# Ten products over a blank tile, in place of twenty, ahead of the first dense product of a two-layer encoder kernel

## The chip, the core and the metric

One core of one Trainium2 chip runs the whole program. The metric is the device time of one execution, in microseconds (us), as the median of several runs.

## The reference, cut to what matters

One sequence of 512 tokens of width 1024 goes through two layers. The first is a Mamba-2 mixer (a state-space scan in chunks), the second a differential attention. The change lies ahead of the first layer's first projection. What is computed there and right behind it is this:

```python
h = rms_norm(x, norm_g)
zxbcdt = h @ w_in                       # z, then x/B/C, then dt
z, xbc, dt_raw = ...
xbc = jax.nn.silu(causal_depthwise_conv(xbc, conv_w, conv_b))
dt = jax.nn.softplus(dt_raw + dt_bias)
y = ssd_chunked_scan(xs * dt[..., None], -jnp.exp(a_log) * dt, bm, cm)   # cumsum of a*dt, exp of its differences
y = gated_group_rms_norm(y + d_skip * xs, z, gate_norm_g)
x = x + y @ w_out
```

Everything is float32. The second layer (a shared K/V projection, eight heads of attention with two softmax maps each, an output projection, a last norm) isn't touched.

## The kernel before, in words

**Products in three parts.** Each dense product is made of three in a faster format: both operands are split into a high part and the rest, and TensorE (PE) computes high by high, high by rest and rest by high (`mm3`). ScalarE (ACT) writes the high part of the weights (`whi`) and VectorE (DVE) the rest (`wlo`), in four pieces of 128x512 for each load of weights (`raw`, 1 MB, sent from SyncE's queue). `raw` has two buffers, `whi` and `wlo` three, so the pieces of the sixth load (called raw5 below) can only be written once PE has finished with those of the third. For the input, `a_hi` and `a_lo` are the same two parts of x transposed (`xt`).

**The head of the program.** `blank` is a 128x128 tile of zeros. A loop multiplies it with itself into a PSUM bank that nobody reads (`warm`), while the first weights and inputs are still in transfer; each such product shows as two rows in the trace. Then come the products of `pz0`: four tiles of 128 tokens by 8 slices of the width by 3, 96 in all.

```python
    V.memset(blank, 0.0)
    ...
    warm = ss_bank("warm")
    for i in range(20):
        T.matmul(warm[:, 0:P], lhsT=blank, rhs=blank, start=True, stop=True)
```

**Behind it.** The squares of x give the norm's factors (`scales`, with `ar_col` by token and `ar_row` along a row). `z_out` takes each `pz` bank to SBUF through SiLU (`zs`). A small product, `ps_dt`, gives dt's raw values; then DVE and ACT compute softplus by a series: `pre` (scaled, biased), `e` (its exponential on ACT), `q` and a chain of eight steps on `pl`, then `pre` again, `q` (a times dt) and the cumulative sum along the chunk, a scan into `e`, which the code calls `acs`. From it ACT makes one more exponential (`toe`, in the tile `q`), and SyncE sends it to DRAM and back, spread over all partitions (`acs_d`, then `dec`). GpSimd (POOL) and ACT make the decays of it.

**The first group.** PE goes on with the projection of group 0 (`pg`: four tiles by 8 slices by 3, 96 products, 48 with one load of weights and 48 with the next). Inside it stand three transposes, `ps_tt`, whose operands are `pre`, `acs` and `toe`. Their place in PE's queue is fixed: after 22 steps, 66 products, of group 0.

```python
    def turned():
        yield "tt"
        ps_tt = ss_bank("ps_tt")
        for i, src in enumerate((dtp, acs, toe)):
            T.transpose(ps_tt[:, i * P:(i + 1) * P], src, ident)
    ...
    T.on = True
    resume(0, 0, turned(), {"tt": 22})
    first_layer()
```

A finished `pg` tile goes through `conv`: DVE multiplies by `ar_row`, ACT starts `xc`, DVE adds three shifted products, ACT takes SiLU. `pxt` are transposes of two such results, further back in PE's queue.

**What sets the order.** Each engine works through its own list in order. Where `T.on` (or `V.on`, `A.on`) is set, the list keeps the order of the code. Elsewhere a scheduler chooses the order when the program is built, after times of its own. In the head and in the first layer PE keeps the code's order from `ps_dt` on, while ACT, DVE, SyncE and the first 96 products of PE are the scheduler's to order. So a change of a loop's count can move instructions far from it.

Nearly all lines go through a helper that records each operation, so they stand under L70, and tiles tell them apart.

Of the kernel before, what the change touches and what calls it, by code (L numbers as in the profile page):

```python
# [78 lines left out]
def trunk(ctx, tc, x, x_t, par, w_dt, w_in, w_out, w_kvqg, w_bo, d_skip, lam_qk, fin_g, out):  # L79
# [16 lines left out]
    def ss_bank(name):  # L96
        turns[0] += 1
        tag = "mm" if turns[0] % turns[1] >= 3 else "ss"
        return psum.tile([P, 512], F32, tag=tag, name=name, bufs=3 if tag == "ss" else 4)
# [290 lines left out]


    warm = ss_bank("warm")
    for i in range(20):
        T.matmul(warm[:, 0:P], lhsT=blank, rhs=blank, start=True, stop=True)
    xt = [bp2.tile([P, 2, S], F32, tag="yl", name=f"xt{i}", bufs=4) for i in range(4)]

# [829 lines left out]
```

## Time and profile before

| | us |
|---|---|
| median of 3 runs (707.1 to 707.22) | 707.15 |
| the profiled execution | 707.6 |
| its span, first to last instruction | 705.8 |
| PE busy (share of the span) | 698.2 (99%) |
| DVE busy | 524.3 (74%) |
| ACT busy | 426.8 (60%) |
| POOL busy | 114.9 (16%) |

The span leaves out 1.8 us of the profiled execution that lie around it. A busy share says for which part of the span an engine had an instruction running. PE's rows overlap their neighbours, since a product is still draining when the next begins; so the distance from start to start tells what one costs, and the busy share tells only that PE stood still nowhere for long.

### The profile page before, as it was taken

How to read it: one execution, taken by the hardware profiler on the slowest of the kernel's cores; microseconds unless marked ns; L12 is line 12 of the kernel's file. 1: busy time of each engine (PE TensorE's matmuls, PEld its weight loads, DVE VectorE, ACT ScalarE, POOL GpSimd, SP SyncE). 2: the span in 40 equal slices, each digit the busy share in tenths (PEclk: the TensorE clock that was granted, in tenths of full speed). 3: DMA queues.
4: the chain of work that ended last, by engine and by line, in shares of the span. 5: the costliest groups of instructions: out<-in, count | busy, mean ns of one | idle time of the engine just before them, and what ended most of it. 6: DMA issues, size and time to landing. Idle time of an engine off the chain costs nothing.

```text
span 705.8 us, 10517 instructions
## 1 busy us (share of the span) xinstructions
PE 698.2 (99%) x3861; PEld 584.5 (83%) x3861; DVE 524.3 (74%) x1184; ACT 426.8 (60%) x930; POOL 114.9 (16%) x154
## 2 busy tenths in 40 slices
PE   9999999999999999999999999999999999999996
PEld 8888888888888888888888888888888888888884
DVE  5599957789489679569996757557778757787776
ACT  6859564484653737536635158567777667665546
POOL 0008241602405025042110101000000000000002
PEclk9999999999999999999999999999999999999999
DMA  8653313314024223313123111513112221130003
GB/s 297 254 208 153 123 57 120 119 61 179 23 97 181 72 107 120 110 71 119 60 67 114 60 59 51 197 60 114 66 60 75 79 87 60 60 107 14 30 1 119
DMA packets 13491, 70.85 MB, mean 100 GB/s; under 512 B 1792, under 2 KB 3328, under 8 KB 6016
## 3 DMA queue, kind: packets, MB, share of 16 engines
q1 hardware_dynamic: 13008, 69.90, 27.5%
q8 instruction: 30, 0.49, 0.3%
q10 hardware_dynamic: 432, 0.28, 0.1%
q14 instruction: 21, 0.17, 0.1%
HBM read 68.02 MB, written 2.16 MB: 99 GB/s over the span
## 4 chain that ended last, share of the span: by engine, by line
PE 93%; DVE 2%; ACT 1%; issue 1%; DMA 1%; POOL 1%; ACTq 0%; POOLq 0%; SPq 0%
PE pg L70 21%; PE po L70 16%; PE pz L70 12%; PE pt L70 8%; PE pq L70 6%; PE pk L70 6%; PE pv L70 6%; PE pb L70 3%; PE sc L70 3%; PE pyd L70 2%; PE pc L70 2%; PE warm L70 1%; PE pyt L70 1%; PE pxt L70 1%; PE psA L70 1%
## 5 line engine op out<-in xcount | busy, mean ns | idle before, releaser
L70 DVE SCALAR_TENSOR_TENSOR wlo<-raw,prm,whi 128x512 fp32r<-128x512 f32 (+1 forms) x240 | 149.0, 672 | 52.4 <-ACT whi L70 52.1
L70 ACT ACTIVATE whi<-raw,prm 128x512 fp32r<-128x512 f32 (+1 forms) x240 | 133.2, 629 | 44.8 <-PE pg L70 13.7
L70 PE MATMUL pg<-a_hi,whi 128*128 128x512 f32 x256 | 102.6, 401 | 0.0
L70 PE MATMUL pg<-a_hi,wlo 128*128 128x512 f32 x256 | 99.8, 390 | 0.0
L70 PE MATMUL pg<-a_lo,whi 128*128 128x512 f32 x256 | 99.8, 390 | 0.0
L70 DVE SCALAR_TENSOR_TENSOR xc<-pg,prc,xc 128x511 f32<-128x511 f32 (+2 forms) x96 | 71.1, 745 | 13.0 <-ACT xc L70 11.8
L70 PEld LDWEIGHTS pg<-a_hi,wlo 128*128 128x128 f32 x256 | 48.0, 188 | 10.2
L70 PEld LDWEIGHTS pg<-a_hi,whi 128*128 128x128 f32 x256 | 48.1, 188 | 9.7 <-issue 0.2
L70 PEld LDWEIGHTS pg<-a_lo,whi 128*128 128x128 f32 x256 | 48.1, 188 | 9.4
L70 PE MATMUL po<-whi,yh 128*128 128x512 f32 x128 | 51.2, 400 | 0.0
L70 PE MATMUL pz<-whi,a_hi 128*128 128x512 f32 x128 | 50.5, 396 | 0.0
L70 PE MATMUL po<-whi,yl 128*128 128x512 f32 x128 | 49.9, 390 | 0.0
L70 PE MATMUL po<-wlo,yh 128*128 128x512 f32 x128 | 49.9, 389 | 0.0
L70 PE MATMUL pz<-whi,a_lo 128*128 128x512 f32 x128 | 49.9, 389 | 0.0
L70 PE MATMUL pz<-wlo,a_hi 128*128 128x512 f32 x128 | 49.8, 389 | 0.0
L1031 POOL TENSOR_TENSOR ot<-x_tok,fg 128x512 f32<-128x512 f32 x4 | 5.0, 1299 | 246.9 <-DVE x_tok L70 246.9
L70 ACT ACTIVATE xc<-xc 128x512 f32<-128x512 f32 x32 | 20.2, 631 | 38.3 <-DVE xc L70 34.4
L70 DVE CUSTOM_DVE_ANT_0 s<-sc,bias 128x128 f32<-128x128 f32 (+3 forms) x64 | 29.4, 488 | 16.0 <-PE sc L70 15.5
L70 ACT ACTIVATE s<-s,mx 128x128 f32<-128x128 f32 (+3 forms) x64 | 35.6, 557 | 9.1 <-DVE mx L70 8.9
L70 ACT ACTIVATE xc<-pg,prc 128x512 f32<-128x512 f32 x32 | 24.8, 774 | 26.3 <-DVE pg L70 24.5
L656 POOL TENSOR_TENSOR xe<-xdt,tok 128x256 f32<-128x256 f32 x24 | 14.1, 613 | 159.3 <-DVE xdt L70 159.3
L70 ACT ACTIVATE tmp<-dx 128x256 f32<-128x256 f32 x32 | 13.2, 412 | 44.2 <-DVE dx L70 44.2
(239 smaller groups left out, 1657.7 us busy)
## 6 DMA issues: line engine op xcount, KB each, us to landing
raw<-in_w_in SPq DMA_DIRECT2D x22, 1024.0 KB, 4.9
raw<-in_w_kvqg SPq DMA_DIRECT2D x16, 1024.0 KB, 4.8
dec<-acs_d SPq DMA_DIRECT2D x8, 1024.0 KB, 4.8
raw<-in_w_out SPq DMA_DIRECT2D x8, 1024.0 KB, 4.9
raw<-in_w_bo SPq DMA_DIRECT2D x4, 1024.0 KB, 4.8
x_tok<-in_x SPq DMA_DIRECT2D x4, 512.0 KB, 9.1
out<-ot SPq DMA_DIRECT2D x6, 256.0 KB, 2.1
raw<-in_w_in SPq DMA_DIRECT2D x4, 256.0 KB, 4.7
```

What stands on the lines that cost most here:

```text
L70: i = op(*args, **kw)
L656: GP.tensor_tensor(out=xe[:, c], in0=xdt[:, c], in1=toe_tok[:, c, hs].unsqueeze(2).to_broadcast([P, R, HD]), op=ALU.mult)
L1031: GP.tensor_tensor(out=o, in0=y, in1=f, op=ALU.mult)
```

## The change

The loop over the blank tile runs ten times.

```diff
     warm = ss_bank("warm")
-    for i in range(20):
+    for i in range(10):
         T.matmul(warm[:, 0:P], lhsT=blank, rhs=blank, start=True, stop=True)
```

The scheduler then orders parts of the first layer anew. Numbers behind a name are buffers; those of the changed program are lower by ten (`wlo_498` is now `wlo_488`).

PE, start of the program. Before:

```order
L70 MATMUL warm<-blank 128x128 x20
L70 MATMUL pz_0_140<-whi_138,a_hi 128x512
L70 MATMUL pz_0_140<-wlo_139,a_hi 128x512
L70 MATMUL pz_0_140<-whi_138,a_lo 128x512
L70 MATMUL pz_1_141<-whi_138,a_hi 128x512
L70 MATMUL pz_1_141<-wlo_139,a_hi 128x512
```

Now:

```order
L70 MATMUL warm<-blank 128x128 x10
L70 MATMUL pz_0_130<-whi_128,a_hi 128x512
L70 MATMUL pz_1_131<-whi_128,a_hi 128x512
L70 MATMUL pz_2_132<-whi_128,a_hi 128x512
L70 MATMUL pz_3_133<-whi_128,a_hi 128x512
L70 MATMUL pz_0_130<-wlo_129,a_hi 128x512
```

The first slices now go through the four tiles with one part of the weights before the next part is used. From `ps_dt` on PE's list is the same as before.

DVE, between the first use of `ps_dt` and the first `conv` (`wlo_434` belongs to the fifth load, `wlo_498` to the sixth). Before:

```order
L70 SCALAR_TENSOR_TENSOR wlo_434<-raw_431,prm,whi_433 128x512
L70 TENSOR_SCALAR pre<-pre,prm 128x128
L70 SCALAR_TENSOR_TENSOR wlo_434<-raw_431,prm,whi_433 128x512 x3
...
L70 SCALAR_TENSOR_TENSOR pl<-pl,q_314 128x128 x7
L70 SCALAR_TENSOR_TENSOR pl<-pl,q_310 128x128
L70 SCALAR_TENSOR_TENSOR pre<-pre,pl 128x128
L70 TENSOR_SCALAR q_314<-pre,begin 128x128
L70 SCALAR_TENSOR_TENSOR e_307<-ones,q_314 128x128
L70 SCALAR_TENSOR_TENSOR wlo_498<-raw_495,prm,whi_497 128x512 x4
L70 TENSOR_TENSOR pg_0_443<-pg_0_443,ar_row 128x512
```

Now:

```order
L70 SCALAR_TENSOR_TENSOR wlo_424<-raw_421,prm,whi_423 128x512 x2
L70 TENSOR_SCALAR pre<-pre,prm 128x128
...
L70 SCALAR_TENSOR_TENSOR pl<-pl,q_304 128x128 x6
L70 SCALAR_TENSOR_TENSOR wlo_488<-raw_485,prm,whi_487 128x512
L70 SCALAR_TENSOR_TENSOR pl<-pl,q_304 128x128
L70 SCALAR_TENSOR_TENSOR wlo_488<-raw_485,prm,whi_487 128x512
L70 SCALAR_TENSOR_TENSOR pl<-pl,q_300 128x128
L70 SCALAR_TENSOR_TENSOR wlo_488<-raw_485,prm,whi_487 128x512 x2
L70 SCALAR_TENSOR_TENSOR pre<-pre,pl 128x128
L70 TENSOR_TENSOR pg_0_433<-pg_0_433,ar_row 128x512
L70 TENSOR_SCALAR q_304<-pre,begin 128x128
L70 SCALAR_TENSOR_TENSOR e_297<-ones,q_304 128x128
```

The scan (the last row, into `e`) stood ahead of the four `wlo` of the sixth load and of the first `conv`'s multiplication; it now stands behind all five. `pre` stands one `wlo` further back.

ACT, from the exponential of softplus to `toe` (written into `q`). Before:

```order
L70 ACTIVATE e_307<-pre 128x128
L70 ACT_TABLE_LOAD
L70 ACTIVATE e_307<-e_307 128x128
L70 ACTIVATE whi_497<-raw_495,prm 128x512 x4
L70 ACTIVATE q_310<-e_307 128x128
L70 ACTIVATE xc_519<-pg_0_443,prc 128x512
```

Now:

```order
L70 ACTIVATE e_297<-pre 128x128
L70 ACT_TABLE_LOAD
L70 ACTIVATE e_297<-e_297 128x128
L70 ACTIVATE whi_487<-raw_485,prm 128x512 x4
L70 ACTIVATE xc_509<-pg_0_433,prc 128x512
L70 ACTIVATE q_300<-e_297 128x128
```

`toe` now stands behind the first `conv`'s start. Beside these, ACT takes the last two `zs` before the four `whi` of the fourth load (they stood behind them), some exponentials and SiLUs of the next 20 us change places, and SyncE issues the eighth load of weights before the four `acs_d` and two `dec` transfers (it stood behind them). POOL's list is the same.

## Rows read from the trace of the kernel before

**Rows 1.** The page, part 4: the chain that ended last, by engine.

```profile
PE 93%; DVE 2%; ACT 1%; issue 1%; DMA 1%; POOL 1%; ACTq 0%; POOLq 0%; SPq 0%
```

**Rows 2.** The chain of waits up to 175 us: start us, us, what.

```profile
33.22 15.19 PE pg L70 x66
```

**Rows 3.** Timeline of PE: start us, us, engine line op out<-in, count [idle before].

```profile
1.06 7.64 PE L70 MATMUL warm<-blank 128*128 128x128 f32 x40 [1.06 <-DVE blank L70]
8.46 0.48 PE L70 MATMUL pz<-whi,a_hi 128*128 128x512 f32 x1
...
33.15 0.50 PE L70 MATMUL pg<-a_hi,whi 128*128 128x512 f32 x1
...
48.46 0.27 PE L70 MATMUL ps_tt<-ident,q 128*128 128x128 f32 x1
```

**Rows 4.** Timeline of PE's weight loads (one for each row of rows 3), around 7 us.

```profile
6.99 0.41 PEld L70 LDWEIGHTS warm<-blank 128*128 128x128 f32 x2
7.20 0.30 PEld L70 LDWEIGHTS warm<-blank 128*128 128x128 f32 x2
7.31 0.19 PEld L70 LDWEIGHTS warm<-blank 128*128 128x128 f32 x1
```

**Rows 5.** Timeline of ACT, the first weights.

```profile
4.57 0.72 ACT L70 ACTIVATE whi<-raw,prm 128x512 fp32r<-128x512 f32 x1 [1.90 <-DMA prm<-in_par]
```

**Rows 6.** Timeline of ACT, 31 to 49 us.

```profile
31.25 2.59 ACT L70 ACTIVATE whi<-raw,prm 128x512 fp32r<-128x512 f32 x4
33.70 0.86 ACT L70 ACTIVATE zs<-pz,ar_col 128x256 f32<-128x256 f32 x2
34.41 0.62 ACT L70 COPY ar_row<-aps_r 128x512 f32<-128x512 f32 x1
...
37.35 0.34 ACT L70 ACTIVATE e<-pre 128x128 f32<-128x128 f32 x1
...
44.13 2.57 ACT L70 ACTIVATE whi<-raw,prm 128x512 fp32r<-128x512 f32 x4 [4.82 <-PE pg L70]
46.60 0.39 ACT L70 ACTIVATE q<-e 128x128 f32<-128x128 f32 x1
48.59 0.78 ACT L70 ACTIVATE xc<-pg,prc 128x512 f32<-128x512 f32 x1 [1.60 <-DVE pg L70]
```

**Rows 7.** Timeline of DVE, 36 to 48 us.

```profile
36.96 0.28 DVE L70 TENSOR_SCALAR pre<-pre,prm 128x128 f32<-128x128 f32 x1
37.16 2.07 DVE L70 SCALAR_TENSOR_TENSOR wlo<-raw,prm,whi 128x512 fp32r<-128x512 f32 x3
39.35 0.23 DVE L70 TENSOR_SCALAR q<-e 128x128 f32<-128x128 f32 x1
...
41.51 2.58 DVE L70 SCALAR_TENSOR_TENSOR pl<-pl,q 128x128 f32<-128x128 f32 x8
44.12 0.29 DVE L70 SCALAR_TENSOR_TENSOR pre<-pre,pl 128x128 f32<-128x128 f32 x1
...
44.77 0.42 DVE L70 TENSOR_TENSOR_SCAN e<-ones,q 128x128 f32<-128x128 f32 x1
...
47.86 0.70 DVE L70 TENSOR_TENSOR pg<-pg,ar_row 128x512 f32<-128x512 f32 x1
```

**Rows 8.** Timeline of ACT, the first decays and the SiLU behind them.

```profile
61.00 1.93 ACT L70 ACTIVATE dec<-dec 128x2056 f32<-128x2056 f32 x1 [0.56 <-POOL dec L616]
...
64.24 0.64 ACT L70 ACTIVATE xc<-xc 128x512 f32<-128x512 f32 x1
```

**Rows 9.** The tile pxt, 60 to 75 us: durations, first and last start.

```profile
L70 PE MATMUL pxt<-ident,xc x8: 270/272/273, 68.9 to 69.7; 128*128 128x128 f32 x8
```

**Rows 10.** The page, part 6: DMA issues, KB each, us to landing.

```profile
raw<-in_w_in SPq DMA_DIRECT2D x22, 1024.0 KB, 4.9
```

**Rows 11.** Busy time by stretch: us, PE, PEld, DVE, ACT, POOL; PEclk, DMA share, GB/s.

```profile
699.00:700.00 1.00, 0.53 (x3) 0.10 (x1) 1.00 (x4) 0.96 (x3) 0.00 (x0) 1.00 0.82 305
...
703.00:704.00 1.00, 0.00 (x0) 0.00 (x0) 0.00 (x0) 0.00 (x0) 0.00 (x0) 0.76 1.01 339
```

## The prediction

> **What bounds the kernel now.** I read the shares of the chain that ended last first: 93% of it is PE [rows 1]. So a microsecond that PE gains or loses in its queue should reach the end, unless some later wait of PE takes it back. Next comes PE's timeline at the head: the blank products, 40 rows for 20 products, run from 1.06 us, and the first real product starts at 8.46 [rows 3]. Its weights (`whi`) were ready at 4.57 + 0.72 = 5.29 [rows 5], so PE's own queue kept it waiting for about 3.2 us. That is what the change can take away. Then I look where PE next needs something that is not set by PE's own progress. The first such place is the three transposes `ps_tt`: the third, of `toe`, starts at 48.46 [rows 3], and `toe` was done at 46.60 + 0.39 = 46.99 [rows 6]. So it was 1.5 us early. That cover is the number to watch, because the lists of DVE and ACT that make `toe` are ordered anew.
>
> **What the change takes away.** Ten products are 20 rows. Around 7 us the rows first follow each other at 0.21 us (6.99 to 7.20) and then at 0.11 us (7.20 to 7.31) [rows 4]: PE ran at its lower level until 7.20 and at its higher from there, though it had worked without a pause from 1.06. With 20 rows left the blank products end at 1.06 + 20 x 0.21 = 5.3, just when the first weights are ready. A real product costs 15.19 / 66 = 0.230 us at the higher level [rows 2], so about 0.230 x 0.21 / 0.11 = 0.44 at the lower. If the level rises at 7.2 again, four products run slowly, from 5.3 to 7.1, and the fifth starts at 7.1. Before it started at 8.46 + 4 x 0.23 = 9.4. **PE's gain at the head is 2.3 us.** It isn't 20 x 0.21 = 4.2, since the slow stretch is now filled with real work. The products of the first slices are now ordered by part of the weights, which needs `wlo` and `a_lo` later, so the new order costs nothing.
>
> PE then reaches group 0 at 33.15 - 2.3 = 30.85 in place of 33.15 [rows 3] and the transposes after 66 products, at 30.85 + 15.19 = 46.0 [rows 2].
>
> **What the new order adds.** Does the chain to `toe` come earlier as well? Its start is `ar_row`, at 34.41 on ACT, behind four `whi` and two `zs` [rows 6]. In the new order the same four and two stand there, swapped; none of the six was waiting for PE in the trace, and the rows around them follow without a pause. So `ar_row` stays at 34.41 although PE is 2.3 us ahead. From there I go down the new list of DVE:
>
> - `pre` stood at 36.96 and now stands behind one more `wlo`, 2.07 / 3 = 0.69 us: it starts at 37.65 and ends at 37.93. ACT's exponential, at 37.35 before [rows 6], starts about then, 0.6 later, and `q` moves from 39.35 to 39.95 [rows 7].
> - The chain of `pl` starts at 41.51 + 0.6 = 42.1. Its steps follow each other every (44.12 - 41.51) / 8 = 0.326 us; six take it to 44.07.
> - Then come four `wlo` of the sixth load (4 x 0.69 = 2.76) with the last two `pl` and `pre` between and behind them. A small step that waits for none just before it takes 37.16 - 36.96 = 0.20 [rows 7], so three take 0.6. The multiplication of the first `conv` starts at 44.07 + 2.76 + 0.6 = 47.4 and ends 0.70 later, at 48.1. The `whi` that these `wlo` need were released by PE at 44.13 before [rows 6]; 2.3 earlier is 41.8, early enough.
> - `q` and the scan follow: 48.1 + (44.77 - 44.12) / 2 = 48.45, and the scan ends at 48.9. Before it ended at 44.77 + 0.42 = 45.2. It is **3.7 us later**.
> - ACT now takes the start of the first `conv` before `toe`: from 48.15 for 0.78 [rows 6], so `toe` runs from 48.9 to 49.3.
>
> So the third transpose starts at about 49.35, where it was at 48.46: **0.9 us later than before**. PE arrives at 46.0 and stands for 3.3 us, less two short transposes. The gain of 2.3 is lost there and 0.9 more. Everything behind it on PE's queue comes 0.9 later, and as PE has next to no idle time from there to the end, nothing gives it back.
>
> Bounds of this term: if the three small steps hid wholly under the `wlo` it would be 0.9 - 0.6 = 0.3; if they cost 0.326 each, 0.9 + 0.4 = 1.3. I take 0.9, from the row with the same pattern (a small step between two `wlo`).
>
> **What lies behind the transposes.** `acs` also goes through DRAM to POOL and ACT. ACT's first decay exponential stood at 61.00 and was waiting for POOL [rows 8], so it moves by the scan's 3.7 to 64.7. SyncE's eighth load now stands ahead of `acs_d`; such a load takes 4.9 us to land [rows 10] and can go out once the fourth `wlo` is done, near 47.2, so it lands near 52.1 and can hold `acs_d` (issued from 48.9) by perhaps a microsecond: 65.7. The second SiLU for `pxt` now follows the decays directly: 64.24 - 61.00 = 3.24 behind, and 0.64 long [rows 8], so it is done at 68.6 to 69.6. PE takes the eight `pxt` between 68.9 and 69.7 before [rows 9]; the second four, from 69.3, move to 70.2. Cover left: 0.6 to 1.6 us. I cost it at nothing.
>
> **The sum.** The profiled execution, 707.6, minus 2.3 plus 3.2 gives 708.5. Its own time stands 0.45 above the median of the runs, 707.15; on that median the forecast is 707.15 + 0.9 = 708.05, given as **708.1**. Its own range is 707.4 to 708.5. A measurement of this kernel can tell about 0.2%, 1.4 us, from no change, so this counts as no change.
>
> **The rivals.**
>
> *The clock falls in the new wait.* PE would stand for 3.3 us in the middle of its work. What the trace shows of such a fall is at its end: PE's last product ran into the stretch 699 to 700, half busy, so until about 699.5; the granted clock was still 1.00 there, and in 703 to 704 it averages 0.76, which is the higher level for half of that stretch and the lower for the rest [rows 11]. The fall came some 4 us after the last product, longer than the 3.3 here, and here two transposes lie in between. That speaks against it; that the two lengths are so near speaks for some chance. The price: at the start PE worked at the lower level for 7.2 - 1.06 = 6.1 us, at half the rate, so a fall costs up to 3.1 us: 708.05 + 3.1 = 711.1, slower. Chance 0.17.
>
> The Trainium skill, page "TensorE: Matmul & The Clock Gate", section "Why this matters for your kernels", advises against idle gaps between bursts of products, since the clock then returns to its lower level; by that rule the time would be this rival's 711. The trace shows one such gap, and the clock outlasted most of it.
>
> *The gain stays.* If the scan were not late (DVE faster through the new order than its rows say, or ACT reaching `ar_row` earlier), PE would keep its 2.3 us: 707.15 - 2.3 = 704.85. It decides at 46.0: `toe` would have to be ready 3.3 us sooner than I work out. The swapped order and the count of five instructions of 0.69 or 0.70 ahead of the scan speak against it. Chance 0.08.
>
> *A second wait.* If the decays come more than 0.6 to 1.6 us later than worked out, PE stands again at `pxt`, and DVE, which multiplies the decays in order, pushes work back. With one more microsecond lost: 709.1. Chance 0.13.
>
> That the change doesn't do what it says can be left out: the rows are in the list, ten for twenty.
>
> **How the numbers follow.** Forecast 0.62, clock 0.17, second wait 0.13, gain 0.08. Slower by over 0.2% (above 708.6): all of the clock case, two thirds of the second wait, and about a tenth of the forecast for errors in a long sum: 0.17 + 0.09 + 0.06 = 0.32. Faster by over 0.2%: 0.08. Within: 0.60. The range goes from 707.0 (a little under the lower bound of the forecast) to 710.3 (most of the clock case, as a fall may cost less than its full price); it leaves out the gain and the top of the clock case.
>
> **What would show it.** The first real product near 5.3 and its neighbours at 0.44 apart until about 7.2; group 0 starting near 30.9; `ar_row` still near 34.4; the scan ending near 48.9; idle time of PE of some 3 us at `ps_tt`, ended by DVE and ACT; the next `pg` product about 0.9 later than before, and that shift unchanged at the end. Wrong would be: no idle time at `ps_tt`; products behind it at 0.44 apart; idle time at `pxt`.

## The result, and the profile after

| | before | changed |
|---|---|---|
| median of 6 runs each, us | 707.03 (706.05 to 707.22) | 710.58 (709.89 to 713.59) |
| the profiled execution, us | 707.6 | 709.89 |
| its span, us | 705.8 | 708.1 |
| PE busy, share of the span | 99% | 98% |

Over all runs the ratio is put at 1.006, with an interval of 1.0042 to 1.0078 (the medians alone give 1.0050): by the medians the change makes the kernel **slower by 3.5 us**. The two profiled executions differ by 2.3 only, since the one of before lies 0.57 over the median, above all six of its runs, and the one of the change is its fastest (0.69 under the median): 2.29 + 0.57 + 0.69 = 3.55. Differences between two traces below are to be read with that in mind.

The chain that ended last (the page of the changed kernel, part 4) is still PE's, as in [rows 1]:

```profile
PE 95%; DVE 2%; ACT 1%; DMA 1%; issue 0%; SPq 0%; ACTq 0%
```

PE's timeline of the changed kernel (start us, us, engine line op out<-in, count [idle before]) answers to [rows 3]:

```profile
1.06 4.21 PE L70 MATMUL warm<-blank 128*128 128x128 f32 x20 [1.06 <-DVE blank L70]
5.31 1.20 PE L70 MATMUL pz<-whi,a_hi 128*128 128x512 f32 x4
6.35 1.08 PE L70 MATMUL pz<-wlo,a_hi 128*128 128x512 f32 x4
...
9.38 0.73 PE L70 MATMUL pz<-whi,a_hi 128*128 128x512 f32 x2 [0.59 <-ACT a_hi L70]
...
30.95 0.50 PE L70 MATMUL pg<-a_hi,whi 128*128 128x512 f32 x1
...
45.82 0.39 PE L70 MATMUL pg<-a_hi,wlo 128*128 128x512 f32 x1
47.93 0.33 PE L70 MATMUL ps_tt<-ident,pre 128*128 128x128 f32 x1 [1.72 <-DVE pre L70]
49.30 0.48 PE L70 MATMUL ps_tt<-ident,e 128*128 128x128 f32 x1 [1.05 <-DVE e L70]
49.76 0.47 PE L70 MATMUL ps_tt<-ident,q 128*128 128x128 f32 x1
49.88 0.77 PE L70 MATMUL pg<-a_hi,whi 128*128 128x512 f32 x1
50.45 0.63 PE L70 MATMUL pg<-a_lo,whi 128*128 128x512 f32 x1
50.88 0.63 PE L70 MATMUL pg<-a_hi,wlo 128*128 128x512 f32 x1
...
52.53 0.40 PE L70 MATMUL pg<-a_hi,whi 128*128 128x512 f32 x1
```

Four things stand in it. At the head the first four real products take 1.04 us (5.31 to 6.35), 0.26 each, and at 9.38 PE stands for `a_hi`. Group 0 starts at 30.95, 2.20 earlier than at 33.15. The third transpose starts at 49.76, 1.30 later than at 48.46: PE stood twice for `pre` and the scan's `e`, 1.72 and 1.05 us. And the products right behind it follow each other at 0.43 us (50.45 to 50.88) until 52.53, from where they stand at 0.24 and less. Six products take 52.53 - 49.88 = 2.65 us; at the 0.230 of [rows 2] they would take 1.38. That is 1.27 more.

The granted clock by stretches of 1 us in the changed kernel (us, PE, PEld, DVE, ACT, POOL busy; PEclk, DMA share, GB/s) shows why:

```profile
48.00:49.00 1.00, 0.26 (x1) 0.06 (x1) 0.96 (x3) 0.36 (x1) 0.00 (x0) 1.00 0.54 66
49.00:50.00 1.00, 0.69 (x3) 0.43 (x3) 0.80 (x2) 0.70 (x2) 0.00 (x0) 0.52 0.53 197
50.00:51.00 1.00, 1.00 (x4) 0.81 (x4) 0.93 (x3) 0.14 (x1) 0.00 (x0) 0.50 1.02 434
...
52.00:53.00 1.00, 1.00 (x4) 0.77 (x4) 0.27 (x1) 0.00 (x0) 0.00 (x0) 0.77 0.19 49
```

The clock fell from 1.00 (2.4 GHz) to 0.50 (1.2 GHz) at about 49.0, inside the wait, and rose again in the middle of 52 to 53. From there PE runs 1.30 + 1.27 = 2.6 late and stays so: the first `pcb`, at 62.21 before, starts at 64.81, and the end comes 2.3 later.

DVE's timeline of the changed kernel, 38 to 49 us, answers to [rows 7]:

```profile
38.25 0.28 DVE L70 TENSOR_SCALAR pre<-pre,prm 128x128 f32<-128x128 f32 x1
...
40.53 0.23 DVE L70 TENSOR_SCALAR q<-e 128x128 f32<-128x128 f32 x1 [0.68 <-ACT e L70]
...
47.90 0.70 DVE L70 TENSOR_TENSOR pg<-pg,ar_row 128x512 f32<-128x512 f32 x1
...
48.83 0.42 DVE L70 TENSOR_TENSOR_SCAN e<-ones,q 128x128 f32<-128x128 f32 x1
```

The scan starts at 48.83 where it started at 44.77. What hangs on it besides the transposes goes through SyncE, POOL and ACT. SyncE's issues in the kernel before, and then in the changed one (start us, us, queue):

```profile
45.22 1.74 SPq L476 DMA_DIRECT2D acs_d<-e  x4
48.10 0.81 SPq L611 DMA_DIRECT2D dec<-acs_d  x2
```

```profile
49.28 1.73 SPq L476 DMA_DIRECT2D acs_d<-e  x4
53.51 0.82 SPq L611 DMA_DIRECT2D dec<-acs_d  x2
```

and the first decay exponential on ACT in the changed kernel, with the SiLU behind it, which answers to [rows 8]:

```profile
66.74 1.93 ACT L70 ACTIVATE dec<-dec 128x2056 f32<-128x2056 f32 x1 [1.64 <-POOL dec L616]
...
69.98 0.63 ACT L70 ACTIVATE xc<-xc 128x512 f32<-128x512 f32 x1
```

`acs_d` goes out 4.06 later, `dec` 5.41 later, and the exponential comes 5.74 later than at 61.00. In this trace PE never stands for it: beside the two waits at `ps_tt` and two ahead of 10 us (1.1 us for the blank tile and the 0.6 for `a_hi`), no wait of PE is listed at all. Whether it costs anything could not be read from this trace; it took the experiments.

### The profile page after: what moved, and what is told of

The parts are those of the page before. It is cut to its first block, busy times and chain, and to the rows that moved or that the text cites. A ratio compares the mean times of both kernels' runs of the same rounds, so it can differ in the third digit from the quotient of the medians.

```text
span 708.1 us, 10475 instructions
## 1 busy us (share of the span) xinstructions
PE 697.3 (98%) x3841; PEld 582.0 (82%) x3841; DVE 524.3 (74%) x1184; ACT 427.3 (60%) x930; POOL 114.4 (16%) x154
## 4 chain that ended last, share of the span: by engine, by line
PE 95%; DVE 2%; ACT 1%; DMA 1%; issue 0%; SPq 0%; ACTq 0%
PE pg L70 24%; PE po L70 16%; PE pz L70 12%; PE pt L70 7%; PE pq L70 6%; PE pv L70 6%; PE pk L70 6%; PE pb L70 3%; PE sc L70 3%; PE pyd L70 2%; PE pc L70 2%; PE pyt L70 1%; PE pcb L70 1%; PE pxt L70 1%; PE psA L70 1%; DMA xt<-in_x_t 1%
## 5 line engine op out<-in xcount | busy, mean ns | idle before, releaser
L70 PE MATMUL pz<-whi,a_hi 128*128 128x512 f32 x128 | 48.7, 397 | 0.6 <-ACT a_hi L70 0.6
L70 PE MATMUL pz<-wlo,a_hi 128*128 128x512 f32 x128 | 48.2, 389 | 0.0
L70 PE MATMUL pz<-whi,a_lo 128*128 128x512 f32 x128 | 48.1, 390 | 0.0
```

The source lines that it names most:

```text
L70: i = op(*args, **kw)
```

## The experiments

Two readings had to be told apart, and then a third. (1) All of it is **the wait** at `ps_tt`: its length and the clock that falls in it. (2) Part of it is **the late scan's other end**, the decays. (3) The shorter loop itself costs something, whatever the order. The kernels differ from before by what the short diffs show and by the count of blank products; the scheduler then orders some instructions behind these edits anew. `issue_after(x)` puts an instruction behind x in its engine's list. All medians are in us; "before" is the kernel before, run beside it on the same chip. The ratio is over all runs, so it can differ a little from that of the two medians. The recorded expectations speak of theories: A is reading 1, B is reading 3, and C, D and E are forms of reading 2. They also name later steps of PE on the first group; in PE's order these are `pcb`, `pbt`, `pxt`, `psA`, `pyd`, `po` and `pyt`.

| kernel | blank products; what else | median (before) | ratio [interval] |
|---|---|---|---|
| e1_scan_first | 10; scan ahead of the sixth load's `wlo` | 706.50 (706.68) | 1.0002 [0.9993, 1.0010] |
| e2_fill_wait | 10; 8 products ahead of the transposes | 710.59 (706.68) | 1.0055 [1.0041, 1.0068] |
| e3_seventeen | 17 | 706.26 (706.68) | 0.9998 [0.9989, 1.0007] |
| e4_eleven | 11 | 709.74 (706.68) | 1.0049 [1.0037, 1.0062] |
| e5_fill_all | 10; 9 and 4 products fill the wait | 710.33 (706.51) | 1.0053 [1.0040, 1.0067] |
| e6_order_only | 20; scan and `toe` late | 710.59 (706.51) | 1.0056 [1.0044, 1.0069] |
| e7_thirteen_scan_first | 13; scan ahead | 705.79 (706.51) | 0.9988 [0.9980, 0.9997] |
| e8_ten_again | 10 (the changed kernel) | 710.03 (706.51) | 1.0059 [1.0045, 1.0073] |
| e9_hop_one | 20; one more DRAM tile to `acs_d` | 709.82 (706.05) | 1.0053 [1.0041, 1.0065] |
| e10_fill_acs_first | e5; eighth load behind `acs_d` | 709.85 (706.05) | 1.0054 [1.0042, 1.0066] |
| e11_acs_first | 10; eighth load behind `acs_d` | 710.83 (706.05) | 1.0060 [1.0046, 1.0074] |
| e12_hop_two | 20; two more DRAM tiles | 707.48 (706.05) | 1.0016 [1.0007, 1.0025] |
| e13_order_exp_last | e6; decay exponentials moved back | 709.68 (706.42) | 1.0050 [1.0038, 1.0062] |
| e14_ten_exp_last | 10; the same | 711.28 (706.42) | 1.0073 [1.0060, 1.0086] |
| e15_fill_exp_last | e5; the same | 712.36 (706.42) | 1.0083 [1.0070, 1.0096] |
| e16_thirteen_exp_last | e7; the same | 705.77 (706.42) | 0.9993 [0.9984, 1.0002] |
| e17_ten_dec_last | 10; both steps of the decays moved back | 710.03 (706.69) | 1.0050 [1.0036, 1.0064] |
| e18_fill_dec_last | the same, and the wait filled | 708.63 (706.69) | 1.0031 [1.0019, 1.0042] |

### Is it the place of the scan, or the shorter loop?

```diff
+            sixth = fetched[0] == 5
-            with tc.high_priority():
+            with tc.high_priority(), tc.issue_after(scan_end.ins) if sixth else ExitStack():
                 for piece in pieces_:
                     lay(piece)
...
-    for i in range(20):
+    for i in range(10):
...
-    V.tensor_tensor_scan(out=acs, data0=ones, data1=adt, initial=0.0, op0=ALU.mult, op1=ALU.add)
+    scan_end = V.tensor_tensor_scan(out=acs, data0=ones, data1=adt, initial=0.0, op0=ALU.mult, op1=ALU.add)
```

> Ten blank rows, with the pieces of the sixth weight load put behind the scan, so that VectorE has the scan before the four wlo and the pg multiplication as in the kernel before. Theory A (the late scan makes TensorE stand, and the clock falls in that wait): the third ps_tt transpose starts at 46.4 to 47.0 in place of 49.76, no products 0.43 us apart follow, and the time is 705.0 to 705.7 us, some 2 us under the kernel before. Theory B (the fewer blank rows themselves cost it, by a slower start of TensorE): the third transpose is early but the time stays at 709 us or more. Theory C (a later wait, for the first dec or pxt, takes the gain): the third transpose is early, group 0's dec step is waited for, and the time is 706.8 to 708 us.

With ten products and the scan put back ahead of the four `wlo`, the loss is gone: 706.50 against 706.68. PE's timeline of this kernel:

```profile
46.72 0.33 PE L70 MATMUL ps_tt<-ident,e 128*128 128x128 f32 x1 [0.45 <-DVE e L70]
47.15 0.33 PE L70 MATMUL ps_tt<-ident,q 128*128 128x128 f32 x1
...
54.57 0.47 PE L70 MATMUL pg<-a_hi,whi 128*128 128x512 f32 x1 [0.24 <-DVE xc L70]
```

The third transpose now starts at 47.15, 1.31 earlier than before. But only 0.5 of it is left at the end of the span, and next to nothing in the medians (0.18): PE gives some of its lead back in waits, here 0.45 for the scan and 0.24 for an `xc`. Where the rest goes was not followed. So reading 3 falls, and the lead at the head is worth little even where nothing eats it at once.

Kernels that only change the count say the same. With 17 the order of DVE, ACT and SyncE is that of before, with 11 that of the change:

```diff
-    for i in range(20):
+    for i in range(17):
```

> Seventeen blank rows: the order on VectorE, ScalarE and SyncE is that of the kernel before, so only the head term is left, three of the ten rows. Theory A: TensorE reaches group 0 at 32.4 to 32.9 in place of 33.15, the time is 706.3 to 706.8 us, 0.3 to 0.7 under the kernel before. Theory B (fewer blank rows slow the start): 707.2 us or more.

> Eleven blank rows: the order on VectorE, ScalarE and SyncE is that of the changed kernel, TensorE's lead is about 0.2 us smaller. Theory A: TensorE stands 3.0 to 3.3 us at ps_tt, the products behind are 0.43 us apart for some 2 us, the time is 710.0 to 711.0 us. If the wait is now just short enough to keep the clock: 0.23 us apart, 708.2 to 708.6 us. Theory B: 709.8 to 710.2 us, a tenth of the loss less.

706.26 and 709.74. Seventeen products gain nothing that can be measured, and eleven lose nearly what ten lose.

The other way round: twenty products, with the scan and `toe` put where the changed kernel has them.

```diff
-    V.tensor_tensor_scan(out=acs, data0=ones, data1=adt, initial=0.0, op0=ALU.mult, op1=ALU.add)
-    acs_d = tc.dram_tile([H, NQ, P], F32, name="acs_d")
-    for c in range(NQ):
-        nc.sync.dma_start(acs_d[:, c, :], acs[c * H:(c + 1) * H, :])
...
+    def scan(mult, first):
+        with tc.high_priority():
+            with tc.issue_after(mult.ins):
+                V.tensor_tensor_scan(out=acs, data0=ones, data1=adt, initial=0.0, op0=ALU.mult, op1=ALU.add)
+            for c in range(NQ):
+                nc.sync.dma_start(acs_d[:, c, :], acs[c * H:(c + 1) * H, :])
+            with tc.issue_after(first.ins):
+                A.activation(toe, acs, AF.Exp, scale=-1.0, bias=acs[:, P - 1:P])
```

Here `mult` is the first `conv`'s multiplication on DVE and `first` its start on ACT.

> Twenty blank rows as before, but the scan pinned behind the four wlo of the sixth weight load and the pg multiplication, and the toe activation behind the first xc, as they stand in the changed kernel. Theory A (order gives the delay at ps_tt, the lead of TensorE only makes the wait long enough to lose the clock): first transpose at 48.2 to 48.4, third at 49.4 to 49.9, TensorE idle some 1.2 us, no fall of the clock, time 707.9 to 708.7 us (1.2 to 1.6 over the kernel before). Rival (the order is enough for the whole loss): the clock falls here too, products 0.43 us apart, 709.3 to 710.6 us. Rival (the lead alone does it): no change, 706.5 to 707.2 us.

710.59: the order alone, with no product taken away, costs what the change costs. Its waits of PE (for whom, us in total, times, longest):

```profile
PE pyt L70 <- ACT tmp L70: 1.3, 1, 1.3
...
PE ps_tt L70 <- DVE e L70: 0.5, 1, 0.5
PE ps_tt L70 <- ACT q L70: 0.5, 1, 0.5
```

PE stands at `ps_tt` for only 1.0 and the clock never falls. The third transpose starts at 49.26, 0.8 late, and `pcb` 0.84 late. But then PE loses again: by its start times against before's it is 1.55 late at group 0's first `po` (85.76 for 84.21) and 3.15 at the first `pyt` (108.26 for 105.11), where it stands 1.3 for ACT. **So there is a loss behind the transposes that reading 1 does not know.** The late scan is enough for the whole loss (this kernel) and needed for it (e1).

### The wait and its clock

```diff
         for i, src in enumerate((dtp, acs, toe)):
+            for _ in range((9, 4, 0)[i]):
+                T.matmul(ps_tt[:, 3 * P:4 * P], lhsT=ident, rhs=ident, start=True, stop=True)
             T.transpose(ps_tt[:, i * P:(i + 1) * P], src, ident)
```

The products go into a part of the bank that nobody reads. The first form, e2, has eight of them ahead of the first transpose and none behind it.

> Ten blank rows, and eight 128x128 products of the identity matrix with itself into a free part of the ps_tt bank, ahead of the three transposes; the order on every other engine is that of the changed kernel. They fill about 1.8 us of the 3.5 us that TensorE has between its last pg product and the third transpose. Theory A (clock): the third transpose stays at 49.5 to 49.9, the products behind it are 0.23 us apart from the start, and the time is 708.2 to 708.8 us. Rival (the wait's length is all, the clock is no cause of its own): nothing changes, 710.2 to 711.2 us. If 1.8 us of filling does not hold the clock, the products behind are 0.43 us apart as in the changed kernel and the time is 710.2 to 711.2 us too, which the spacing tells apart.

710.59, and the clock fell all the same: its stretches read 0.92 in 49 to 50, 0.50 in 50 to 53. The eight were done by 47.2 and PE stood from there. The second form fills both parts of the wait.

> Ten blank rows, and identity products in the whole of the wait at ps_tt: nine ahead of the first transpose, four between the first and the second. Up to the third transpose every other engine has the changed kernel's order (behind it four VectorE rows and two ScalarE rows stand a place or two elsewhere). Theory A (TensorE's standing lowers the clock): the third transpose starts at 49.5 to 50.0 as in the changed kernel, the granted clock stays 1.00, the products behind are 0.23 us apart, the first pbt stands at 64.2 to 64.6 (63.10 before, 65.70 changed), and the time is 707.9 to 708.7 us. Rival (the late scan costs the rest by itself, through VectorE and ScalarE behind it): the clock stays 1.00 but the first pbt or a later mark is at +2.3 us all the same, and the time is 709.5 us or more.

PE's timeline of e5:

```profile
45.97 2.17 PE L70 MATMUL ps_tt<-ident 128*128 128x128 f32 x18
47.98 0.27 PE L70 MATMUL ps_tt<-ident,pre 128*128 128x128 f32 x1
48.09 1.06 PE L70 MATMUL ps_tt<-ident 128*128 128x128 f32 x8
49.19 0.33 PE L70 MATMUL ps_tt<-ident,e 128*128 128x128 f32 x1
49.64 0.33 PE L70 MATMUL ps_tt<-ident,q 128*128 128x128 f32 x1
49.73 0.48 PE L70 MATMUL pg<-a_hi,whi 128*128 128x512 f32 x1
50.04 0.39 PE L70 MATMUL pg<-a_lo,whi 128*128 128x512 f32 x1
```

The products behind the wait stand 0.23 apart again and the clock reads 1.00 throughout. **The kernel is not faster for it:** 710.33. PE's start times against those of before tell where the saving goes (us later; minus is earlier):

| | third `ps_tt` | first `pcb` | first `pyt` | second group's `pxt` | end of span |
|---|---|---|---|---|---|
| before, start | 48.46 | 62.21 | 105.11 | 110.11 | 705.8 |
| changed | +1.30 | +2.60 | +2.61 | +2.82 | +2.3 |
| e5 (filled) | +1.18 | +1.23 | +2.19 | +3.11 | +2.5 |
| e6 (order alone) | +0.80 | +0.84 | +3.15 | +4.05 | +3.5 |
| e17 (decays back) | +1.63 | +3.26 | +3.26 | +3.26 | +2.6 |
| e18 (both) | +1.42 | +1.49 | +1.50 | +1.70 | +1.1 |

Without the slow clock PE loses 1.9 us between the first `pcb` and the second group's `pxt`, in small pieces: the eight `pyt`, for example, take 1.95 us where they took 1.04 before (it is for ACT's `tmp`, which they transpose, that PE stands in e6).

```profile
107.30 1.95 PE L70 MATMUL pyt<-ident,tmp 128*128 128x128 f32 x8
```

With the slow clock PE is late enough to lose next to nothing there (+2.60 to +2.82). Two delays seem to lie side by side, each covering the other; that had still to be tried. From the second group's `pxt` to the end all five come back by 0.5 to 0.7, since there before itself loses 0.7: its second run of `pyt`, at 150.79, takes 1.55 us, where the others take 0.87.

> The changed kernel once more, beside the others on one chip. Theory A: third transpose at 49.3 to 49.9, granted clock 0.50 for 2.5 to 3.5 us from about 49, time 709.7 to 711.5 us; any profile whose clock does not fall there should be about 1.3 us shorter.

The changed kernel again: 710.03 against 706.51, with the clock low from about 51.0 to 54.4 in this execution. So here the clock outlasted the whole wait, and fell when PE had been at work again since 49.39 (the stretch 50 to 51 still reads 0.98, and 51 to 54 read 0.50).

### Late decays alone

In the kernel before, with its twenty products and its early scan, `acs` goes through one more DRAM tile on its way to `acs_d` (e9), or two (e12).

```diff
+    hops = [tc.dram_tile([H, NQ, P], F32, name=f"hop{i}") for i in range(1)] + [acs_d]
     for c in range(NQ):
-        nc.sync.dma_start(acs_d[:, c, :], acs[c * H:(c + 1) * H, :])
+        nc.sync.dma_start(hops[0][:, c, :], acs[c * H:(c + 1) * H, :])
+    for a, b in zip(hops, hops[1:]):
+        nc.sync.dma_start(b[:], a[:])
```

> The kernel before, twenty blank rows and the scan in its place, but its result passes through one more DRAM tile before acs_d, so that the first dec load is issued later and behind a weight load, as in the changed kernel. TensorE has no wait at ps_tt and the clock has no reason to fall. Theory D (the late scan costs by the way scan, acs_d, dec, POOL, exp, pyd, and not at ps_tt): the first dec step on POOL starts 2.5 to 4.5 us later than 52.68, TensorE loses 1 to 3 us between psA and the second pxt, time 707.5 to 709.5 us. Theory A (the wait at ps_tt and the clock are the loss): no change, 706.2 to 707.0 us.

709.82, though PE takes the transposes 1.5 earlier than before and stands for none of them. POOL gets `dec` at 58.23 (58.07 in the changed kernel, 52.68 before). ACT's timeline of e9, the waits of PE, and the clock by stretches of 1 us behind that wait:

```profile
66.48 1.92 ACT L70 ACTIVATE dec<-dec 128x2056 f32<-128x2056 f32 x1 [4.67 <-POOL dec L619]
...
70.75 0.63 ACT L70 ACTIVATE xc<-xc 128x512 f32<-128x512 f32 x1
```

```profile
PE pxt L70 <- ACT xc L70: 3.5, 1, 3.5
```

```profile
72.00:73.00 1.00, 1.00 (x5) 0.77 (x5) 0.96 (x3) 0.78 (x1) 0.84 (x2) 0.59 0.00 0
73.00:74.00 1.00, 1.00 (x4) 0.81 (x3) 1.00 (x2) 0.98 (x1) 0.00 (x0) 0.50 0.00 0
...
75.00:76.00 1.00, 1.00 (x4) 0.76 (x4) 1.00 (x3) 1.00 (x1) 0.00 (x0) 0.70 0.00 0
```

ACT stands 4.67 us for the decays, and the SiLU that PE's `pxt` needs stands in the list behind them. PE waits 3.5 for it, and here too the clock falls: PE's starts go from 1.53 early at the first `pcb` to 3.75 late at `psA`, 5.3 us in all, 3.5 by the wait and 1.8 behind it, where products ran at the lower level. So **late decays, with no wait at `ps_tt`, cost as much as the change**, though PE meets them at another place and in part through the clock. ACT's list is not quite that of before here: one SiLU that stood behind the exponential now stands ahead of it. The Trainium skill, page "TensorE: Matmul & The Clock Gate", section "Architectural detail: the array is 16× 32×32, not 1× 128×128", says that ACT's and DVE's queues are strictly first in, first out; the trace agrees, with 4.67 us of ACT standing while a later step of its list held up PE.

> As the run with one more DRAM tile, but with two: the first dec step on POOL another 2 to 3 us later. Theory D: another 1.5 to 3 us on the time of that run, 709.5 to 712 us. Theory A: 706.2 to 707.0 us.

Two tiles delay `dec` further, to 59.13 on POOL, and yet cost only 1.4 us (707.48). The scheduler gave this kernel another order, which ACT's timeline shows:

```profile
65.25 0.63 ACT L70 ACTIVATE xc<-xc 128x512 f32<-128x512 f32 x1 [0.28 <-DVE xc L70]
...
67.20 1.92 ACT L70 ACTIVATE dec<-dec 128x2056 f32<-128x2056 f32 x1
```

The SiLU stands ahead of the exponential, which finds its data ready. So the lateness of `dec` is not enough by itself; how much it costs depends on what stands behind it in the lists.

### Attempts to take the second delay out

First by the transfer: the eighth load of weights, which the change put ahead of `acs_d` on SyncE, behind it again (e10 with the wait filled, e11 without).

```diff
-            nc.sync.dma_start(raw.rearrange("p k n -> p (k n)"), src)
+            with tc.issue_after(acs_out.ins) if i == 7 else ExitStack():
+                nc.sync.dma_start(raw.rearrange("p k n -> p (k n)"), src)
```

> The run with the filled wait (ten blank rows, thirteen identity products, clock held), and the eighth weight load's transfer issued behind the acs_d writes instead of ahead of them. Theory D: dec is issued at about 52.0 in place of 53.3, the first dec step on POOL starts at 56.2 to 56.8 in place of 57.7, TensorE's mark at the second pxt falls from +3.1 to +1.2 to +2.2, time 708.0 to 709.4 us. If the weight transfer, now later, is what counts: 710 us or more.

> The changed kernel with the eighth weight load's transfer issued behind the acs_d writes; the wait at ps_tt is not filled. If wait with lowered clock and late dec are two delays side by side, each some 2 us, the one that is left holds the time: clock 0.50 behind ps_tt, first pbt at +2.4 to +3.0, time 709.4 to 710.4 us. If the late dec alone is the loss: 708.0 to 709.2 us.

709.85 and 710.83. With the load behind them the four `acs_d` were quick again: in e10 `dec` was issued at 52.11, 1.15 us after the last `acs_d`, where that takes 2.50 in the changed kernel and 1.14 before. But the load, issued at 51.05, now went out between `acs_d` and `dec`, and POOL's first step on `dec` came at 58.50 (57.68 in e5) and 59.05 (58.07 in the changed kernel), later and not earlier. The delay moved from one transfer to the next; the decays did not come sooner, so these two decide nothing.

Then by ACT's list: the two exponentials of the first decays behind the last SiLU of group 0.

```diff
-        A.activation(xc, xc, AF.Silu)
+        last = A.activation(xc, xc, AF.Silu)
+        if ft == 1:
+            with tc.issue_after(last.ins):
+                held.pop()()
```

> Twenty blank rows with the scan and toe where the changed kernel has them (the run of the order alone, 710.59 us), and the two exp of dec put behind group 0's last silu on ScalarE. Theory E (the loss behind ps_tt is ScalarE standing for the late dec with the silu queued behind): the fourth silu no longer waits, TensorE's marks stay at their offset of the first pcb to the second pxt (within 1 us), time 707.0 to 708.4 us. If the late dec itself holds TensorE, through pyd, whatever the queue: 709.5 us or more.

> The changed kernel, with only the two exp of dec put behind group 0's last silu. If the wait at ps_tt with its slow clock (+2.6 us at the first pbt) and ScalarE's order are two delays side by side, the first alone still holds the time: clock 0.50 for some 3 us, 709.2 to 710.4 us. If ScalarE's order is the whole loss: 707.0 to 708.6 us.

> Both delays taken out of the changed kernel: the wait at ps_tt filled with thirteen identity products (clock held), and the two exp of dec behind group 0's last silu. Two delays side by side: clock 1.00, first pbt at +1.0 to +1.4 against the profile of the kernel before, no loss above 1 us up to the second pxt, time 707.2 to 708.6 us, where either remedy alone gives 709.5 us or more. If something third holds it: 709.5 us or more.

> Thirteen blank rows, the scan in its old place (705.79 us before), and the two exp of dec behind group 0's last silu. Theory E: the loss of 1 us between the first pcb and psA that the form with the scan alone showed is gone, time 704.6 to 705.6 us. If the later dec costs as much at pyd: 705.6 to 706.6 us.

Counted from the kernel before beside it, e13 gains 0.8 on e6 (3.3 over before in place of 4.1); e14 (711.28) and e15 (712.36) lose 1.3 and 2.1 more than the same kernels without the move, and e16 stays at 705.77, e7's time. (In e15 PE stands 1.3 for POOL's `xe` at group 0's `psA`, and the clock falls behind that, to 0.73 on the mean of 80 to 85.) DVE's timeline of e13 shows where the delay went:

```profile
69.78 2.48 DVE L70 TENSOR_TENSOR dec<-dec,pcb 128x512 f32<-128x512 f32 x4 [4.00 <-ACT dec L70]
72.18 0.74 DVE L70 SCALAR_TENSOR_TENSOR xc<-pg,prc,xc 128x511 f32<-128x511 f32 x1
```

Now DVE stands, 4.00 us, at the multiplication by `pcb`, with the next `conv` behind it. Moving one of the two steps moved the stand from one list to the next; in e14 and e15 DVE stands 4.0 at the same place.

### Both steps moved, with and without the wait filled

```diff
+        last = A.activation(xc, xc, AF.Silu)
+        if ft == 17:
+            with tc.issue_after(last.ins):
+                held.pop()()
...
+            with tc.issue_after(conv_end[17].ins) if g == 0 else ExitStack():
               V.tensor_tensor(out=dec[:, h], in0=dec[:, h], in1=pcb.rearrange("p (c l) -> p c l", l=P), op=ALU.mult)
```

The exponentials go behind group 1's first SiLU, the multiplications behind its first `conv`. e18 also has the 9 and 4 products of e5.

> The changed kernel with both steps that wait for dec moved back in their queues: the two exp behind the first silu of group 1 on ScalarE, the multiplications by pcb behind group 1's first conv on VectorE. The wait at ps_tt is as in the changed kernel. Two delays side by side (the queues behind dec; the wait with the slow clock): only the second is left, first pbt at +2.4 to +3.0 against the profile of the kernel before, time 709.0 to 710.4 us. Queues alone: 707.2 to 708.6 us.

> As the run before it, with the wait at ps_tt filled by thirteen identity products. Two delays side by side: both are gone, clock 1.00, first pbt at +1.0 to +1.5, no more than 1.2 us lost from there to the second pxt, time 707.2 to 708.8 us, at least 1 us under the run before it and under the filled run without the move (710.33 us). If dec holds TensorE whatever the queues: 709.6 us or more.

The waits of PE, first in e17, then in e18:

```profile
PE ps_tt L70 <- DVE pre L70: 2.4, 1, 2.4
...
PE ps_tt L70 <- DVE e L70: 1.0, 1, 1.0
```

```profile
PE ps_tt L70 <- DVE pre L70: 0.3, 1, 0.3
PE ps_tt L70 <- DVE e L70: 0.2, 1, 0.2
```

The four medians side by side:

| | wait as it is (clock falls) | wait filled (clock holds) |
|---|---|---|
| decays as changed | 710.58 and 710.03 | 710.33 |
| both steps moved back | 710.03 | 708.63 |

Taking out either delay alone gains next to nothing; taking out both gains. All six runs of e18 (708.22 to 709.74) lie below all five of e17 (709.82 to 710.77), which ran beside them. By their edits e18 and e5 differ only in the two moved steps, and the times by 1.7 us. Their lists differ further, though: with the move the scheduler also put a later decay exponential ahead of the last `tmp` on ACT (98.62 in e18, 102.78 in e5), and some of DVE's steps on `hst` and `dx` ahead of the last steps of a `conv`. That exponential stands right where e5 is late at `pyt`. So the 1.7 us belong to the move together with what the scheduler made of it; no run parts the two. What is left, 1.94 over the kernel before, fits the late third transpose: in e18's trace it is 1.42 late and the end 1.1, and the profiled execution of before, against which this is counted, lies 0.9 above the median of before in these runs.

### Thirteen products with the scan ahead

> Thirteen blank rows and the scan pinned ahead of the sixth load's wlo; up to the first conv VectorE and ScalarE have the order of the kernel before. TensorE reaches group 0 at 31.4 to 31.9 (33.15 before). If the lead can be kept where the order is unchanged: third transpose at 46.9 to 47.4, no fall of the clock, time 705.0 to 705.9 us. If VectorE (weight splits and conv steps, whose start is set by the weight transfers and not by TensorE) bounds this stretch: the transposes are early, TensorE waits for xc at the fourth product group or later marks fall back to under 0.7 us of lead, and the time is 706.0 to 706.9 us.

Thirteen blank products with e1's scan: 705.79, ratio 0.9988. It is faster than before by 0.7 us, by an interval that ends at 0.9997: a small gain, below the 0.2% that was named as the bound, and e16, which has the same count and the same place of the scan, does not confirm it beyond its interval (1.0002). Its profile shows PE 2.37 earlier at the first transpose and 0.93 earlier from `psA` of group 0 on: over half of the lead is taken back on the way, 0.8 of it in a wait for `xc` at `pxt`.

## Why the prediction was wrong

**Right in number, partly by luck: the head.** "PE's gain at the head is 2.3 us" measured 2.20 in this pair of executions (30.95 for 33.15), with the blank rows ending at 5.27 and the first product at 5.31. The way there was another. The first four products were to stand 0.44 apart; they stood 0.26 apart, which saves some 0.7. And the new order was to cost nothing; but the 15th product came at 9.38, some 0.7 later than at the usual distance behind the two that start from 8.17, because `a_hi` had to wait for x. ACT's timeline of the changed kernel:

```profile
8.92 0.41 ACT L70 CAST a_hi<-xt 128x256 fp32r<-128x256 f32 x1 [1.21 <-DMA xt<-in_x_t]
```

The two errors cancel. In e5, e10 and e15 the four products took 1.72 to 1.86, as forecast, and PE did not stand for `a_hi`. The base was unlucky too: group 0 starts at 33.15 in the trace of before and between 31.62 and 32.59 in the other four traces with twenty products, on the mean of five at 32.2; in the eleven traces with ten it starts at 30.6 on the mean. So the usual gain is about 1.6. `ar_row` was to stay at 34.41 and came at 34.70.

**Right: the lateness of the scan.** It was to start at 48.45 and end at 48.9; it started at 48.83 and ended at 49.25. `toe` was to start at 48.9 and started at 49.32. That this eats the whole lead at `ps_tt` is what happened.

**Undersized: the third transpose, "0.9 us later than before".** It was 1.30, the upper bound. The predicted start of `q`, 39.95, came at 40.53: `pre` slipped 1.29 and not 0.69, and DVE then stood 0.68 for ACT's `e`. The lists were counted rightly and the waits between them too low.

**Wrong, but hidden in this result: "I cost it at nothing".** It asked only whether the second SiLU would be in time for the first `pxt`, and there it was right: PE stood at that `pxt` neither here nor in e5. In the changed kernel's trace the decays cost PE next to nothing (+2.60 to +2.82). What was missed is that late decays hold up what stands behind them in ACT's and DVE's lists, so that a loss can appear 20 to 45 us later, at `po`, `pyt` and the next `pxt`: in e5 and e6, where the clock holds, 1.9 and 3.2 us from the first `pcb` to the second group's `pxt`. The decays themselves were forecast at 64.7 to 65.7 and came at 66.74: `dec` went out 5.41 late where the scan was 4.06 late, as the four `acs_d` took longer beside the eighth load (2.50 us from the end of their issue to `dec`, 1.14 before; 1.15 in e10, where the load stood behind them).

**Wrong: the wait costed by its length alone.** This is the step that failed in the result. The rival in which the clock falls got 0.17, since at the end of before the clock outlasted the last product by some 4 us [rows 11], more than the wait. Here it fell 2.8 us after the last `pg` ended (46.21 to 49.04), with one transpose in between. Nor would outlasting the wait have been enough: in e8, the same kernel, it fell 5.0 us after the last `pg` ended, with PE at work again. Its price was set at up to 3.1; it measured 1.27 in this execution. "Products behind it at 0.44 apart" had been named as a sign of being wrong, and they stood at 0.43. The Trainium skill, page "TensorE: Matmul & The Clock Gate", section "Why this matters for your kernels", advises against gaps between bursts of products, as the clock then returns to its lower level: the trace agrees that it does. But holding the clock (e5) brought nothing as long as the second delay stood beside it, which the page's rule would not have told.

So the lateness of the scan held, and the sum failed by one term that was too small, the third transpose (+0.4), and by two that were set to zero: the clock (+1.3) and the decays (hidden behind the clock here, 1.9 and 3.2 us in two kernels that hold it). The measured 710.58 lies 2.5 above the forecast of 708.1, and just above the range. For the profiled execution the prediction gave 708.5, and 709.89 came. These 1.4 are the 0.4 and the 1.3, less some 0.3 on the way, where before itself loses time later. The rest of the 2.5 lies outside the two traces: 0.45, which the prediction took off because the profiled execution of before stands above its median, and 0.69, by which that of the change lies under its own.

**Still open.** In the changed kernel it can't be said how the loss divides: with either cause taken out, nearly all of it stays. That e5's small losses come from the first decays is likely by e18 against e5, but not shown, since the scheduler moved a later exponential too; through which steps of ACT and DVE each of them comes was not followed. Nor did any run bring `dec` forward with the scan left late.

## What to carry to other kernels

An edit that only changes a count can make a scheduler move an instruction behind five others elsewhere; read the new lists of every engine, and follow what the moved instruction feeds to the end of each branch, through DMA and POOL too. A late result can cost not only where it is awaited first, but through all that stands behind the waiting step in a list that works in order; moving one such step back handed the stand to the next engine here. When PE has to wait, don't price the wait by its length alone, and look at the spacing of the products behind it even where the clock outlasts the wait. And if removing one cause of a loss gains nothing, that doesn't clear it: take out both suspects in one kernel before judging either.

## What the hardware showed that was not expected

- The delay from PE's last work to the fall of the clock was not one number. From the end of the last product ahead of the wait to the fall it was 2.8 us in the changed kernel, 3.3 in e4, 3.5 in e14, 4.5 in e11, 4.6 in e17 and 5.0 in e8, all with one or more transposes in between; 2.7 in e2, after fill products that ended at 47.18; 4.2 in e9, where PE had last worked at 67.97 and the clock fell near 72.2; and about 4 at the end of before [rows 11]. In e2, e8, e9, e11 and e17 PE was at work again when it fell, so the wait was paid at the full clock and the work behind it at the lower.
- The price of such a fall at `ps_tt`, from the third transpose to the first `pcb`, was 1.27 to 1.30 us where it came inside the wait (the changed kernel, e4, e14) and 1.63 to 1.66 where it came with PE at work again (e2, e8, e11, e17). Where the clock held, the same stretch lost 0.04 to 0.07.
- The moment at which the clock rises at the head varies between executions of the same 40 blank rows. They took 7.64 us in before [rows 3], 7.07 in e6, 6.23 in e12 and, from PE's timeline, in e9:

```profile
1.06 6.08 PE L70 MATMUL warm<-blank 128*128 128x128 f32 x40 [1.06 <-DVE blank L70]
```

  So the head of the kernel before has 1.5 us of its own from one execution to the next, and a gain of 2 us at the head that is read from one pair of traces is uncertain by nearly as much. The column of the granted clock reads 1.00 in 0 to 5 us all the while, where the rows stand 0.21 apart, twice their later distance. So the level at the head, here and in the prediction, is read from the spacing of the rows alone; the column does not show it.
